# Eight gate tiles of a hybrid decoder layer computed in earlier stages and kept in DRAM instead of in the last stage

## The chip, the cores and the metric

The kernel runs on one core of a Trainium2 chip. The metric is the device time of one execution in microseconds (us), lower is better. One execution in each set is taken with the hardware profiler; its rows are what the argument below rests on.

## What is computed

One inference step of one layer for 520 tokens (a prompt of 512 and 8 samples), model width 1024, everything in float32. The reference, cut to what matters:

```python
x = layer_norm(x_in, ln_in_g, ln_in_b)
xm, ig, fg, og, zm, rcols, zr, u, zs, gm = split_cols(x @ w_in)
y_A = mlstm(xm, ig, fg, og) * silu(zm) @ w_bm     # chunkwise, 4 heads of 256
y_B = rwkv7(rcols) * silu(zr) @ w_br              # 16 heads of 64, state by token
y_C = glu(gelu(s5(u))) * silu(zs) @ w_bs          # 64 groups of 64 complex states
g0, g1, g2 = split(sigmoid(gm), 3)
x = layer_norm(ALPHA * x + (g0 * y_A + g1 * y_B + g2 * y_C) @ w_out, ln_g, ln_b)
```

The change is about `g0`, the merge gate of the mLSTM branch: 1024 of the columns of `x @ w_in`, in eight tiles of 128 columns.

## The kernel before, in words

**Products.** A float32 product is made of three matmuls on split operands: `x` is kept as `xh` + `xl` and a weight tile as `whi` + `wlo`, and the terms hi x hi, lo x hi and hi x lo are added in PSUM. A tile of 128 output columns by 520 tokens is 8 slices of the inner dimension x 3 terms x 2 token halves (256 and 264) = 48 matmuls. `inproj(c0, evac)` makes one tile of `x @ w_in` so. `load_w` fetches the tile in two halves (`wraw`, three buffers); ACT rounds each half to `whi` (L130), DVE takes the rest as `wlo` (L131). `whi` and `wlo` have two buffers.

**Stages.** The program runs RWKV (to about 727 us), S5 with the RWKV output branch beside it (to about 940 us), mLSTM with the S5 output branch beside it (to about 1203 us), then the last stage: gating of the mLSTM output, the product with `w_bm`, and `final()` with the product by `w_out` and the closing layer norm (L1652 ff.). A generator of one stage is interleaved with that of another by `interleave`; within this, a scheduler that works on its own model of time sets the order of the instructions on each engine, and each engine then runs its list in that order. All loads and stores are issued by one queue, SP (SyncE), also in a fixed order: a transfer that waits for its buffer or its data holds up all that are behind it.

**Kept products ("fills").** RWKV's chain over chunks of the prompt leaves PE waiting, so tiles of `x @ w_in` that later stages need are computed there ahead of time: 44 of them stand in the list `fills`. `fill_z` runs `inproj`, copies the tile from PSUM to `zf` (DVE, one copy for each token half) and stores it in DRAM (`zsave`, 260 KB a tile). 25 are made between other products of RWKV; the other 19 are issued at the end of `rwkv()` by `e.fill(len(e.fills))` (L796) and the scheduler spreads them from there.

**The users.** `Merge.gate` (L1551) has two ways: if its columns stand in `zsave` it loads the tile by DMA and applies Tanh, otherwise it calls `inproj`. In the last stage `Merge.other(0, ahead=True)` calls it for the eight tiles of `g0`, which are not among the 44, so they are computed there, on PE, each tile between two columns of the gating: `zz` (kept `zm`) is loaded, `th` = Tanh, `yb` (the mLSTM output, `hmsave`) is loaded, multiplied and split into `w_bmh` and `w_bml`, the operands of the product with `w_bm`. That product needs all eight columns. Its result is scaled by the gate (`gt`, L1587, DVE) and added to `mg` (L1588, POOL).

**xh and xl.** These hold the normalised input for as long as a tile of `x @ w_in` is still to be made. After that the last stage loads the raw normalised rows into the same memory (`xr`, `xg`, from `xsave`, 2 MB) and scales them on POOL for the residual (L1682, ten instructions of 1024 columns).

**Names on the path of RWKV's end.** `cr`, `cy`: matmuls of the chain over the eight chunks; `hm`, `hv`: means and variances of the head norm behind it; `bv`: its result, stored as `ybsave`. S5 then loads `pk`, `uu`, `br`, `cc`, and its first DVE instruction is `bb<-br,pk` (L1000). At S5's end `ss` (DVE) is the last state, `ys` (PE) the last output product, `yssave<-yo` its store, and the S5 branch loads it again as `yb` and splits it into `ysh` and `ysl`.

Of the kernel before, what the change touches and what calls it, by code (L numbers as in the profile page):

```python
# [8 lines left out]
F32 = mybir.dt.float32  # L9
# [6 lines left out]
P = 128  # L16
# [3 lines left out]
N = T + NB  # L20
# [12 lines left out]
EH = math.exp(-0.5)  # L33

C_XM, C_IG, C_FG, C_OG, C_ZM = 0, 1024, 1028, 1032, 2056
C_RC, C_ZR, C_U, C_ZS, C_GM = 3080, 6280, 7304, 8328, 9352


@with_exitstack
def hybrid_step(ctx: ExitStack, tc: tile.TileContext, I, O):  # L40
# [225 lines left out]
    hmsave = dr.tile([KT, P, N], F32, name="hmsave")  # L266
    ud = dr.tile([KT, P, SL, 80], F32, name="ud")
    flc = ExitStack()
    fl = flc.enter_context(tc.tile_pool(name="fl", bufs=1))
    zsave, fills = {}, []  # L270

    def fill_u(ct):
        us = fl.tile([P, SL, 80], F32, tag="fl", bufs=2, name="us")
# [41 lines left out]
    for ct in range(2):  # L315
        fills.append((fill_z, (C_GM + D + ct * P, zd[ct])))

    def fill(k=1):
        for _ in range(k):
            if fills:  # L320
                f, c = fills.pop(0)
                f(c)
# [36 lines left out]

    env = dict(locals())  # L360
    rwkv(tc, I, O, env)
    flc.close()
    mrg = Merge(tc, I, O, env)
    weng[:] = [V, V]
    mrg.open("mr", 1, 4)
    interleave(s5(tc, I, O, env), mrg.other(1), 1.5)
    mrg.pctx.close()
    weng[:] = [V, V]
    mrg.open("ms", 1, 4)
    interleave(mlstm(tc, I, O, env), mrg.s5(), 0.42)  # L370
    mrg.pctx.close()
    mrg.open("mf", 3, 5)
    for _ in mrg.other(0, ahead=True):
        pass
# [6 lines left out]
def interleave(a, b, n):  # L381

    due = 0.0
    for _ in a:
        due += n
        while due >= 1:
            next(b, None)
            due -= 1
    for _ in b:
        pass  # L390


def rwkv(tc, I, O, env):
# [239 lines left out]
    def chain(cts, st):  # L633
        yr = rq.tile([P, 2, T], F32, tag="yr", bufs=1, name="yr")
        st_fin = rq.tile([P, 2, RD], F32, tag="stf", bufs=1, name="stf")
        yv, t1, lr, pcs = st["yv"], st["t1"], st["lr"], st["pc"]
        xv = rq.tile([P, 2, 2, RD], F32, tag="xv", bufs=2, name="xv")
        for pi in range(2):
            G.memset(xv[hs(pi), pi], 0.0)
        for n in range(NCH):  # L640
            b1, b2 = pc("cr"), pc("cy")
            q3 = lambda b, j: b[:, 128 * j:128 * j + 128].rearrange("p (c t) -> p c t", c=2)
            pr_, psa_, py, psn = q3(b1, 0), q3(b1, 1), q3(b2, 0), q3(b2, 1)
            if n < NCH - 1:
                nxv = rq.tile([P, 2, 2, RD], F32, tag="xv", bufs=2, name="xv")
            for pi in range(2):
                G.tensor_copy(xv[hs(1 - pi), pi], yv[hs(1 - pi), pi, :, n, :])  # L647
            for ci, pi in heads:
                mm(pr_[hs(pi), ci, :], st["ar"][ci][:, pi, n, 0:CH], xv[:, pi, ci, :])
            rs = rss[n % 2]  # L650
            A.activation(rs[hs(0), 0], pr_[hs(0)], AF.Copy)
            V.tensor_copy(rs[hs(1), 1], pr_[hs(1)])
            for ci, pi in heads:
                mm(psa_[hs(pi), ci, :], t1[:, :, ci * NCH + n], rs[:, pi, ci, :])
            V.tensor_copy(yv[hs(0), 0, :, n, :], psa_[hs(0)])
            A.copy(yv[hs(1), 1, :, n, :], psa_[hs(1)])
            for ci, pi in heads:
                mm(psn[hs(pi), ci, :], st["bkt"][ci][:, pi, n, :], yv[:, pi, ci, n, :])
            for ci, pi in heads:
                dst = nxv[hs(pi), pi, ci, :] if n < NCH - 1 else st_fin[hs(pi), ci, :]  # L660
                V.scalar_tensor_tensor(dst, xv[hs(pi), pi, ci, :], pcs[ci][hs(pi), n:n + 1], psn[hs(pi), ci, :],  # L661
                                       op0=ALU.mult, op1=ALU.add)
            for ci in range(2):
                for pi in range(2):
                    mm(py[hs(pi), ci, :], xv[:, pi, ci, :], st["ar"][ci][:, pi, n, CH:2 * CH], stop=False)
                for pi in range(2):
                    mm(py[hs(pi), ci, :], yv[:, pi, ci, n, :], lr[:, pi, ci * NCH + n, :], start=False)
            A.activation(yr[:, :, n * CH:(n + 1) * CH], py, AF.Copy)
            if n < NCH - 1:
                xv = nxv  # L670
        for ci in range(2):
            p = pc("wf")
            tr(p[0:64, 0:P], st_fin[:, ci, :])
            wo = rq.tile([64, P], F32, tag="wo", bufs=1, name="wo")
            V.tensor_copy(wo, p[0:64, 0:P])
            for pi in range(2):
                dma(O[10][0, 0, 2 * cts[ci] + pi], wo[:, 64 * pi:64 * pi + 64])
        return yr
# [114 lines left out]
    V.tensor_tensor(yst, yst, lng, op=ALU.mult)  # L793
    V.tensor_tensor(bf, bf, yf, op=ALU.add)
    dma(e.ybsave[:, :, T:N].rearrange("c p b -> p c b"), bvs)
    e.fill(len(e.fills))  # L796
    ctx2.close()
    ctx.close()
    e.weng[:] = [V, V]
# [145 lines left out]
def s5(tc, I, O, env):  # L945
# [20 lines left out]
    for pi in range(KT // 2):  # L966
# [48 lines left out]
        for j in range(2):  # L1015
            c0 = g0 + 8 * j
            eb = sp.tile([P, 8, SL, SC], F32, tag="eb", bufs=2, name="eb")
            et = sp.tile([P, 8, SL, SC], F32, tag="et", bufs=2, name="et")
            pw = lambda t, q, lo_: t[:, q, lo_:lo_ + SL, c0:c0 + 8].rearrange("p s g -> p g s").unsqueeze(3).to_broadcast(sh)
            bx = lambda q: bb[:, q, 8 * j:8 * j + 8].unsqueeze(2).to_broadcast(sh)  # L1020
            V.tensor_tensor(eb, pw(pf, 0, 0), bx(0), op=ALU.mult)
            V.tensor_tensor(et, pw(pf, 1, 0), bx(1), op=ALU.mult)
            V.tensor_tensor(eb, eb, et, op=ALU.add)
            gm = sp.tile([P, 8, SL, SC], F32, tag="gm", bufs=2, name="gm")
            cx = lambda q: ca[:, j, q].unsqueeze(2).to_broadcast(sh)
            V.tensor_tensor(gm, pw(pf, 0, 1), cx(0), op=ALU.mult)
            gt = sp.tile([P, 8, SL, SC], F32, tag="et", bufs=2, name="gt")
            V.tensor_tensor(gt, pw(pf, 1, 1), cx(1), op=ALU.mult)
            V.tensor_tensor(gm, gm, gt, op=ALU.add)


            p = pa("ko")
            for m in range(4):
                mm(p[32 * m:32 * m + 32, 0:2 * P], ca[:, j, 0, 2 * m:2 * m + 2, :].rearrange("p g c -> p (g c)"),
                   eb[:, 2 * m:2 * m + 2].rearrange("p g s c -> p (g s c)"))
            kt = sp.tile([P, 2, P], F32, tag="w4", bufs=6, name="kt")
            A.activation(kt.rearrange("p h c -> p (h c)"), p[:, 0:2 * P], AF.Copy)
            p = pa("kt")
            for h in range(2):
                tr(p[:, h * P:(h + 1) * P], kt[:, h])  # L1040
            for h in range(2):
                A.activation(ko[:, j].rearrange("p (m h c) -> p m h c", h=2, c=SC)[:, :, h],
                             p[:, h * P:(h + 1) * P].rearrange("p (m h c) -> p m h c", h=2, c=SC)[:, :, h], AF.Copy)
            gms.append(gm)
            ebs.append(eb)
        kf = ko.rearrange("p j c -> p (j c)")
        V.tensor_tensor(kf[0:SC], kf[0:SC], dm.rearrange("p g c -> p (g c)"), op=ALU.add)
        for t in range(SL):
# [695 lines left out]
```

## Time and profile before

| | |
|---|---|
| median of 3 runs | 1374.99 us |
| lowest, highest | 1374.82, 2058.82 us |
| profiled execution | 1377.44 us |
| span of its trace | 1375.5 us |
| matmul engine (PE) busy | 1248.1 us, 91% of the span, 10509 instructions |
| VectorE (DVE) busy | 990.8 us, 72% |
| ScalarE (ACT) busy | 643.8 us, 47% |
| GpSimd (POOL) busy | 241.5 us, 18% |
| mean granted clock of PE | 0.953 of full speed |

The highest of the three runs stands far off from the other two, which differ by 0.17 us; the median is beside the lower ones. The profiled execution is 2.45 us above the median. Busy shares are means over stages that have different limits, so the stages are read apart: by windows of the trace, by the chain of waits that ends last, and by the timeline of a single engine.

### The profile page before, as it was taken

How to read it: one execution, taken by the hardware profiler on the slowest of the kernel's cores; microseconds unless marked ns; L12 is line 12 of the kernel's file. 1: busy time of each engine (PE TensorE's matmuls, PEld its weight loads, DVE VectorE, ACT ScalarE, POOL GpSimd, SP SyncE). 2: the span in 40 equal slices, each digit the busy share in tenths (PEclk: the TensorE clock that was granted, in tenths of full speed). 3: DMA queues.
4: the chain of work that ended last, by engine and by line, in shares of the span. 5: the costliest groups of instructions: out<-in, count | busy, mean ns of one | idle time of the engine just before them, and what ended most of it. 6: DMA issues, size and time to landing. Idle time of an engine off the chain costs nothing.

```text
span 1375.5 us, 27646 instructions
## 1 busy us (share of the span) xinstructions
PE 1248.1 (91%) x10509; PEld 1141.7 (83%) x10509; DVE 990.8 (72%) x2245; ACT 643.8 (47%) x1404; POOL 241.5 (18%) x396
## 2 busy tenths in 40 slices
PE   4979989998999999999985999996999999999897
PEld 4979988888888888998965889985889888899855
DVE  6795695558567945688936999994776775665857
ACT  4447647364846573342222433333665774453230
POOL 1412211122112221105100002200000012104600
PEclk9989999999998999999977999996999999999999
DMA  6333232222221312354417554464676866475331
GB/s 185 95 109 101 81 97 67 56 63 61 80 77 40 95 55 71 88 170 131 153 44 141 136 104 111 100 160 134 196 230 206 264 201 209 134 218 172 90 110 63
DMA packets 246707, 168.49 MB, mean 122 GB/s; under 512 B 54808, under 2 KB 222106, under 8 KB 246302
## 3 DMA queue, kind: packets, MB, share of 16 engines
q1 hardware_dynamic: 246574, 166.72, 42.9%
q8 instruction: 83, 1.36, 0.4%
q14 instruction: 50, 0.41, 0.1%
HBM read 125.18 MB, written 39.20 MB: 120 GB/s over the span
## 4 chain that ended last, share of the span: by engine, by line
PE 60%; DVE 15%; ACT 8%; DMA 8%; issue 5%; SPq 3%; POOL 0%; DVEq 0%; ACTq 0%
PE g L62 40%; SPq L53 3%; DVE wlo L131 3%; PE ys L62 2%; PE cy L62 2%; PE cr L62 2%; PE qk L62 2%; PE gg L62 1%; PE nd L62 1%; PE s L62 1%; DMA wraw<-in_w_bm_dram 1%; ACT whi L130 1%; PE pn L62 1%; DMA uu<-ud 1%; ACT bk L573 1%
## 5 line engine op out<-in xcount | busy, mean ns | idle before, releaser
L62 PE MATMUL g<-xh,whi 128*128 128x264 f32 (+1 forms) x1552 | 458.5, 296 | 35.8 <-DVE th L1541 14.4
L62 PE MATMUL g<-xl,whi 128*128 128x264 f32 (+1 forms) x1552 | 455.3, 293 | 1.9 <-DVE xl L217 1.9
L62 PE MATMUL g<-xh,wlo 128*128 128x264 f32 (+1 forms) x1552 | 455.0, 293 | 0.6 <-DVE wlo L131 0.4
L62 PEld LDWEIGHTS g<-xh,whi 128*128 128x128 f32 x1552 | 303.1, 195 | 44.5 <-DVE th L1541 15.5
L62 PEld LDWEIGHTS g<-xl,whi 128*128 128x128 f32 x1552 | 303.0, 195 | 4.7 <-DVE xl L217 2.2
L62 PEld LDWEIGHTS g<-xh,wlo 128*128 128x128 f32 x1552 | 302.6, 195 | 4.4 <-DVE wlo L131 1.1
L130 ACT ACTIVATE whi<-wraw 128x512 fp32r<-128x512 f32 x258 | 150.8, 624 | 235.7 <-PE g L62 168.7
L131 DVE TENSOR_TENSOR wlo<-wraw,whi 128x512 fp32r<-128x512 f32 x258 | 201.6, 809 | 56.5 <-ACT whi L130 55.5
L661 DVE SCALAR_TENSOR_TENSOR xv<-xv,pc,cy 64x64 f32<-64x64 f32 x112 | 31.3, 280 | 31.0 <-PE cy L62 28.1
L62 PE MATMUL g<-ysh,whi 128*128 128x256 f32 (+1 forms) x128 | 39.0, 314 | 13.1 <-ACT ysh L258 10.7
L62 PE MATMUL g<-w_bmh,wlo 128*128 128x264 f32 (+1 forms) x128 | 37.3, 293 | 8.2 <-DVE wlo L131 8.1
L599 DVE TENSOR_TENSOR itmp<-lu,xi 128x31 f32<-128x31 f32 (+15 forms) x124 | 42.2, 340 | 2.9
L601 DVE TENSOR_TENSOR xi<-xi,itmp 128x31 f32<-128x31 f32 (+15 forms) x124 | 42.2, 341 | 2.7
L564 DVE TENSOR_TENSOR lr<-gg,maskg 64x256 f32<-64x256 f32 x32 | 13.5, 422 | 42.6 <-ACT la L563 37.3
L647 POOL COPY xv<-yv 64x128 f32<-64x128 f32 x64 | 25.9, 406 | 103.8 <-PE cy L62 56.6
L62 PE MATMUL g<-ysl,whi 128*128 128x256 f32 (+1 forms) x128 | 39.8, 312 | 0.0
L62 PE MATMUL g<-ysh,wlo 128*128 128x256 f32 (+1 forms) x128 | 38.9, 305 | 0.0
L62 PEld LDWEIGHTS g<-ysh,whi 128*128 128x128 f32 x128 | 26.0, 209 | 14.6 <-ACT ysh L258 10.9
L62 PE MATMUL g<-bsh,whi 128*128 128x264 f32 (+1 forms) x128 | 37.8, 301 | 0.0
L62 PE MATMUL g<-bsl,whi 128*128 128x264 f32 (+1 forms) x128 | 37.3, 293 | 0.0
L62 PE MATMUL g<-bsh,wlo 128*128 128x264 f32 (+1 forms) x128 | 37.0, 291 | 0.0
L62 PE MATMUL g<-w_bmh,whi 128*128 128x264 f32 (+1 forms) x128 | 36.9, 289 | 0.0
(583 smaller groups left out, 2948.4 us busy)
## 6 DMA issues: line engine op xcount, KB each, us to landing
wraw<-in_w_in_dram SPq DMA_DIRECT2D x194, 256.0 KB
zsave<-zf SPq DMA_DIRECT2D x36, 260.0 KB
cn<-in_state_mlstm_c_dram SPq DMA_DIRECT2D x32, 256.0 KB
out_dram<-cn SPq DMA_DIRECT2D x32, 256.0 KB
yb<-yssave SPq DMA_DIRECT2D x16, 260.0 KB
zz<-zsave SPq DMA_DIRECT2D x16, 260.0 KB
wraw<-in_w_br_dram SPq DMA_DIRECT2D x16, 256.0 KB
wraw<-in_s_glu_w_dram SPq DMA_DIRECT2D x16, 256.0 KB
```

Source lines behind the costliest of these rows:

```text
L53: nc.sync.dma_start(out, in_)
L62: TE.matmul(out, lhsT, rhs, start=start, stop=stop)
L130: A.activation(hi[:, k, 0:m], raw[:, :, 0:m], AF.Copy)
L131: eng.tensor_tensor(lo[:, k, 0:m], raw[:, :, 0:m], hi[:, k, 0:m].bitcast(F32), op=ALU.subtract)
L564: V.tensor_tensor(lr[hs(pi), pi, u, :], pv[hs(pi), :, 64:128], maskg[hs(pi)].unsqueeze(1).to_broadcast([64, 4, 64]), op=ALU.mult)
L573: A.activation(bk[:, n], bk[:, n], AF.Copy, scale=st["pc"][ci][:, n:n + 1])
L599: V.tensor_tensor(tv, lu[:, s + 1:32, s:s + 1].to_broadcast([P, r, w]), xi[:, s:s + 1, 0:w].to_broadcast([P, r, w]), op=ALU.mult)
L601: V.tensor_tensor(xi[:, s + 1:32, 0:w], xi[:, s + 1:32, 0:w], tv, op=ALU.add)
L647: G.tensor_copy(xv[hs(1 - pi), pi], yv[hs(1 - pi), pi, :, n, :])
L661: V.scalar_tensor_tensor(dst, xv[hs(pi), pi, ci, :], pcs[ci][hs(pi), n:n + 1], psn[hs(pi), ci, :], op0=ALU.mult, op1=ALU.add)
```

## The change

Eight more entries are appended to `fills`, the tiles `C_GM + ct*128` of `g0` with a DRAM buffer `zsave6`. Of the list's last part, all but five tiles are issued at the end of `rwkv()` as before; two more are issued there too, but tied by `tc.issue_after` behind the last matmul of RWKV's chain (`st["last"]`, a `cy<-yv,bkt`); the last three (`LATE`) are issued in S5's companion generator `beside()` after the RWKV branch, tied behind the last transpose of S5's last group (`marks[-1]`). The pool of `zf` stays open until after mLSTM and moves to the right side of the memory. `Merge.gate` is unchanged: its first way is now taken in the last stage.

```diff
+LATE = 3
-    fl = flc.enter_context(tc.tile_pool(name="fl", bufs=1))
-    zsave, fills = {}, []
+    fl = flc.enter_context(tc.tile_pool(name="fl", bufs=1, side="right"))
+    zsave, fills, marks = {}, [], []
+    zd = dr.tile([KT, P, N], F32, name="zsave6")
+    for ct in range(KT):
+        fills.append((fill_z, (C_GM + ct * P, zd[ct])))
     rwkv(tc, I, O, env)
-    flc.close()
-    interleave(s5(tc, I, O, env), mrg.other(1), 1.5)
+    def beside():
+        yield from mrg.other(1)
+        with tc.issue_after(marks[-1]):
+            fill(len(fills))
+        yield
+    interleave(s5(tc, I, O, env), beside(), 1.5)
     interleave(mlstm(tc, I, O, env), mrg.s5(), 0.42)
     mrg.pctx.close()
+    flc.close()
     mrg.open("mf", 3, 5)
@@ rwkv, the chain's step
-                mm(psn[hs(pi), ci, :], st["bkt"][ci][:, pi, n, :], yv[:, pi, ci, n, :])
+                st["last"] = TE.matmul(psn[hs(pi), ci, :], st["bkt"][ci][:, pi, n, :], yv[:, pi, ci, n, :],
+                                       start=True, stop=True)
@@ rwkv, its end
-    e.fill(len(e.fills))
+    e.fill(len(e.fills) - LATE - 2)
+    with tc.issue_after(st["last"].ins):
+        e.fill(2)
@@ s5, for each group
-                tr(p[:, h * P:(h + 1) * P], kt[:, h])
+                last = TE.transpose(p[:, h * P:(h + 1) * P], kt[:, h], e.ident)
+            e.marks.append(last.ins)
```

The number of matmuls stays the same; 384 of them change their place. How the order of instructions moves is shown at three places.

**SP at the end of RWKV.** Before, the queue runs from the last weight loads of RWKV to S5's first loads:

```order
L53 DMA ysb<-ys_d 8x1024
L53 DMA wraw<-in_w_in_dram 128x4x128 x2
L53 DMA ybsave<-bvs 128x8x8
L53 DMA out_dram<-wo 64x64 x4
L53 DMA ybsave<-bv 128x512 x2
L53 DMA pk<-pksave 128x2080
L53 DMA uu<-ud 16x16x80 x8
```

After the change, from the same place on (the stores `zsave_340` are those of the new buffer):

```order
L54 DMA wraw<-in_w_in_dram 128x4x128 x2
L54 DMA out_dram<-wo 64x64 x4
L54 DMA zsave_340<-zf 128x520
L54 DMA wraw<-in_w_in_dram 128x4x128 x2
L54 DMA ybsave<-bv 128x512
L54 DMA zsave_340<-zf 128x520
L54 DMA wraw<-in_w_in_dram 128x4x128 x2
L54 DMA ybsave<-bv 128x512
L54 DMA wraw<-in_w_in_dram 128x4x128 x2
L54 DMA pk<-pksave 128x2080
L54 DMA uu<-ud 16x16x80 x8
```

The load of `pk`, which S5 begins with, now stands behind the stores of kept tiles and behind further pairs of weight loads. On PE the moved matmuls (240 for five tiles) lie as follows: 72 in the sixth of the chain's eight steps (before, these three places held none of them), 128 among the `wf`, `hm` and `hv` matmuls between the chain's last `cy` and the last `hv`, and 40 behind the last `hv`.

**PE at the end of S5.** Before, near the last group's last output products, PE has tiles of the S5 branch (`g<-ysh`) between them:

```order
L62 MATMUL ys<-uu,tm 128x72 x2
L62 MATMUL g<-ysh,whi 128x256
L62 MATMUL g<-ysl,whi 128x256
L62 MATMUL g<-ysh,wlo 128x256
L62 MATMUL g<-ysh,whi 128x256
```

After, in the same place:

```order
L63 MATMUL ys<-uu,tm 128x72 x2
L63 MATMUL g<-xh,wlo 128x264
L63 MATMUL g<-xh,whi 128x264
L63 MATMUL g<-xl,whi 128x264
L63 MATMUL g<-xh,wlo 128x264
```

All 144 matmuls of the three late tiles stand ahead of the last `ys<-ss`, and 38 matmuls of the S5 branch have gone from before it to behind it (52 stood there, now 14). The DVE list has four `wlo` and four `zf` copies more ahead of the last `ss`.

**POOL, the residual's scaling.** Before, its ten instructions stand among the additions `mg<-mg,gt` of the last stage:

```order
L1588 TENSOR_TENSOR mg<-mg,gt 128x256
L1682 TENSOR_TENSOR xr<-xr,xg 128x1024
L1682 TENSOR_TENSOR xg<-xg 8x1024
L1682 TENSOR_TENSOR xr<-xr,xg 128x1024 x3
L1588 TENSOR_TENSOR mg<-mg,gt 128x264
L1682 TENSOR_TENSOR xr<-xr,xg 128x1024
```

After, they stand among the additions `mg<-mg,gth` of the S5 branch, that is, in the mLSTM stage, near the second of its eight tiles:

```order
L1604 TENSOR_TENSOR mg<-mg,gth 128x64x4
L1698 TENSOR_TENSOR xr<-xr,xg 128x1024
L1698 TENSOR_TENSOR xg<-xg 8x1024
L1698 TENSOR_TENSOR xr<-xr,xg 128x1024 x3
L1604 TENSOR_TENSOR mg<-mg,gth 128x64x4
L1604 TENSOR_TENSOR mg<-mg,gth 128x8
L1698 TENSOR_TENSOR xr<-xr,xg 128x1024
L1350 COPY xcs<-xc 128x8
```

Their loads move with them on SP, because `xh` and `xl` are read for the last time at the end of S5's companion work and the last `x @ w_in` tiles of mLSTM and no longer in the last stage. In the last stage PE's list goes from the S5 branch straight to the 384 matmuls with `w_bm` (before: 384 of `x @ w_in`, then these), the first 72 of them ordered by column over three tiles; SP's has the loads `zz`, four `gt`, `yb`, `zz`, four `gt`, `yb` and then `zz` and `yb` in turn, without weight loads of `w_in` between them.

## Rows read from the trace of the kernel before

**Rows 1.** Page, part 1: busy time, share of the span, instructions

```profile
PE 1248.1 (91%) x10509; PEld 1141.7 (83%) x10509; DVE 990.8 (72%) x2245; ACT 643.8 (47%) x1404; POOL 241.5 (18%) x396
```

**Rows 2.** Chain that ended last, its long pieces: start, length (us), what

```profile
1202.75 46.91 PE g L62 x391
...
1310.82 54.77 PE g L62 x254
```

**Rows 3.** Windows by stage: window, length; busy PE, PEld, DVE, ACT, POOL; PEclk, DMA, GB/s

```profile
697.00:740.00 43.00, 26.98 (x210) 20.96 (x208) 12.07 (x35) 12.51 (x34) 4.12 (x9) 0.73 0.41 66
740.00:934.00 194.00, 180.74 (x1613) 172.04 (x1614) 189.91 (x371) 68.42 (x143) 23.36 (x23) 0.94 0.53 120
905.00:940.00 35.00, 32.09 (x272) 30.42 (x270) 29.16 (x72) 11.45 (x23) 0.92 (x4) 0.85 0.43 116
940.00:951.00 11.00, 0.48 (x4) 0.20 (x2) 2.33 (x13) 0.52 (x1) 0.92 (x3) 0.60 0.60 132
1110.00:1130.00 20.00, 20.00 (x137) 17.50 (x139) 18.85 (x60) 13.04 (x29) 3.48 (x6) 1.00 0.65 199
1130.00:1203.00 73.00, 73.00 (x526) 60.76 (x515) 41.29 (x126) 35.42 (x70) 12.50 (x18) 1.00 0.55 173
1250.00:1311.00 61.00, 49.66 (x385) 47.99 (x384) 46.26 (x43) 16.47 (x29) 39.19 (x25) 0.94 0.45 136
```

**Rows 4.** DVE's wlo in 1110 to 1203 us: count, ns min/median/max

```profile
L131 DVE TENSOR_TENSOR wlo<-wraw,whi x14: 684/690/1248, 1115.7 to 1201.6; 128x512 fp32r<-128x512 f32 x14
```

**Rows 5.** DVE's wlo in 1250 to 1311 us: count, ns min/median/max

```profile
L131 DVE TENSOR_TENSOR wlo<-wraw,whi x14: 684/1243/8168, 1250.2 to 1299.7; 128x512 fp32r<-128x512 f32 x14
```

**Rows 6.** Timeline of DVE in the last stage: start, length, instruction, count

```profile
1241.65 0.69 DVE L262 SCALAR_TENSOR_TENSOR w_bml<-yb,w_bmh 128x520 fp32r<-128x520 f32 x1
...
1271.44 0.75 DVE L1587 SCALAR_TENSOR_TENSOR gt<-gt,g 128x256 f32<-128x256 f32 x2
1272.11 11.02 DVE L131 TENSOR_TENSOR wlo<-wraw,whi 128x512 fp32r<-128x512 f32 x2
```

**Rows 7.** Windows of 10 us at the end of RWKV's chain, columns of rows 3

```profile
700.00:710.00 10.00, 6.35 (x76) 5.07 (x74) 3.63 (x14) 1.43 (x6) 0.58 (x2) 0.67 0.06 6
710.00:720.00 10.00, 8.29 (x44) 5.31 (x44) 1.97 (x7) 2.57 (x8) 1.86 (x2) 0.50 0.04 7
```

**Rows 8.** Timeline of PE, end of RWKV: start, length, instruction [idle before]

```profile
722.76 1.13 PE L62 MATMUL hv<-yq,bones 128*128 128x256 f32 x4 [1.72 <-ACT yq L688]
```

**Rows 9.** Timeline of SP's queue, RWKV to S5

```profile
723.05 3.90 SPq L53 DMA_DIRECT2D ybsave<-bv  x2
727.04 0.38 SPq L53 DMA_DIRECT2D pk<-pksave  x1
727.47 5.99 SPq L53 DMA_DIRECT2D uu<-ud  x8
...
735.16 2.83 SPq L53 DMA_DIRECT2D br<-in_s_b_im_dram  x2
```

**Rows 10.** Timeline of DVE, start of S5

```profile
740.23 0.42 DVE L1000 TENSOR_TENSOR bb<-br,pk 128x256 f32<-128x256 f32 x1 [6.38 <-DMA br<-in_s_b_im_dram]
```

**Rows 11.** Timeline of PE, first matmul behind the end of S5

```profile
951.17 0.58 PE L62 MATMUL g<-ysh,whi 128*128 128x256 f32 x1 [10.69 <-ACT ysh L258]
```

**Rows 12.** POOL by line and shape: count, busy us, mean ns, idle before

```profile
L1682 POOL TENSOR_TENSOR xr<-xr,xg 128x1024 f32<-128x1024 f32 x8 | 20.8, 2607 | 0.7 <-DMA xg<-in_ln_in_g_dram 0.7
...
L1682 POOL TENSOR_TENSOR xg<-xg 8x1024 f32<-8x1024 f32 x2 | 4.7, 2356 | 0.0
```

**Rows 13.** Timeline of POOL in the mLSTM stage

```profile
1119.32 1.24 POOL L1588 TENSOR_TENSOR mg<-mg,gth 128x256 f32<-128x256 f32 x1 [2.31 <-DVE r L1282]
```

**Rows 14.** Timeline of SP's queue, start of the last stage

```profile
1204.64 3.96 SPq L53 DMA_DIRECT2D out_dram<-so  x10
...
1209.74 0.45 SPq L53 DMA_DIRECT2D zz<-zsave  x1
```

## The prediction, made from the rows above

> **What bounds the kernel now.** PE is busy for 91% of the span [rows 1], and the change neither adds nor removes a matmul. It moves 384 of them, so the question is what limits each of the stages that give or take them. I read the windows by stage first, then the chain that ended last at the two ends of the change, then the timelines of single engines there.
>
> The last stage gives. Its eight gate tiles are one piece of 46.91 us and 391 matmuls of the chain, 0.120 us each, and nothing but PE is waited for [rows 2]. The product with w_bm follows, and at 1310.82 the product with w_out. That middle window, 1250 to 1311, has 385 matmuls, 46.2 us of work at that rate, but takes 61 [rows 3]; what it loses is seen on DVE: two wlo take 11.02 us, where the same instruction has a median of 0.69 in mLSTM [rows 4 to 6].
>
> Three stages take. At RWKV's end the chain over chunks waits and PE's clock is low: between 700 and 720 PE is busy for 14.64 us of 20 at a granted clock of 0.67 and then 0.50 [rows 7]. S5 from 740 to 934 has DVE busy for 189.91 of 194 us: DVE is its bound [rows 3]. mLSTM has PE busy throughout and, from 1110 to 1130, DVE for 18.85 of 20 [rows 3].
>
> **The change part by part.** All against the profiled execution of 1377.44 us (span 1375.5), which lies 2.45 above the median.
>
> *RWKV's end, five tiles, 240 matmuls, 28.8 us at 0.120.* 200 of them (24.0 us) stand ahead of the last hv, which before ends at 722.76 + 1.13 = 723.9 [rows 8]. What can hide them: PE's idle time of 3.65 + 1.71 us in 700 to 720, the 1.72 us that hv waits [rows 7, 8], and the clock, which steady work would raise: 6.35 x 0.33 + 8.29 x 0.50 = 6.2 us. Together 13.3; so hv ends 10.7 us later. Behind it stands the store of bv, and behind that on SP, now, two more pairs of weight loads and a store ahead of pk; before, pk came 3.99 us after the issue of the bv stores began, with nothing between [rows 9]. A weight load waits for its buffer, which the fifth tile's 40 matmuls behind hv free only as they run, 4.8 us at most; I take 4. Everything that S5 begins with is queued there: pk, eight uu, four br. These take 13.2 us from pk at 727.04 to bb at 740.23, and bb waits for the last of them [rows 9, 10]; they are needed as before, only later. bb then starts near 755. S5 can't catch up, since DVE has 4 us of idle time in 194 [rows 3]: **+15**. Bounds: +8 if the buffers are free and idle time before 700 and after 720 hides a little more; 28.8 if nothing hides. I choose near the low clock's rows, because they lie exactly where the matmuls go.
>
> *S5's end, three tiles, 144 matmuls.* All come before the last ys, 38 of the S5 branch go behind it: 106 x 0.120 = 12.7 us more ahead of it. In 905 to 940 PE has 2.91 us of idle time and loses 32.09 x 0.15 = 4.8 by the clock [rows 3]; 5.0 remain. By DVE it is alike: four wlo at 0.69 [rows 4] and four zf copies, taken like wlo as an upper bound, are 5.5 us ahead of the last ss. The two run beside each other, so I take **+5** (bounds 2 and 12.7). What follows is not shortened: after the last ys the result goes to DRAM and back, and PE's first matmul waits 10.69 us for it [rows 11]. The 38 matmuls that went behind fall into that gap, where PE is busy for 0.48 of 11 us [rows 3], and cost nothing; without the gap they would be 4.6 us. Three zsave stores stand on SP ahead of yssave; a single store's issue takes under 0.5 us, as pk's does [rows 9], and they are in the 5.
>
> *mLSTM, POOL's ten instructions.* They take 20.8 + 4.7 = 25.5 us [rows 12]. Since xh and xl are free earlier, they now follow POOL's mg addition of 1119.32 [rows 13], in the stage where DVE is 94% busy until 1130 and 57% (41.29 of 73) after it, and where PE never waits [rows 3]. In the last stage wlo beside them went from 0.69 up to 8.17 us, and two in a row took 11.02, while two gt, which read PSUM, stayed at 0.75 [rows 4 to 6]. That stage lost 61 - 46.2 = 14.8 us. In mLSTM only the first third falls into the crowded part, and PE's list holds three streams of work to draw on; I take half, **+7**. Bounds: 0, if every stalled DVE result was early enough, and 23.5, if POOL's 25.5 us are lost to DVE less the 1.15 + about 1 us free in the crowded part.
>
> The Trainium skill's page "SBUF — State Buffer", section "SBUF: two separate sides", says that DVE and GpSimd share a port pair, held as an exclusive lock for a whole instruction, and that a DVE operation with two SBUF inputs against a GpSimd operation that reads SBUF blocks fully. The trace agrees: wlo, with two SBUF inputs, has 8.17 us, and gt, with one operand in PSUM, has not [rows 5, 6]. By that rule the move would cost close to the upper bound wherever DVE is the bound, and it speaks against this change: by it the sum would be that of rival B, 1384, by the half that I take 1370.
>
> *Last stage, 46.9 us of matmuls gone.* The time doesn't fall by that, because the product with w_bm needs the gating, which ran beside them: zz is loaded from 1209.74 and the eighth w_bml ends at 1241.65 + 0.69 = 1242.3 [rows 6, 14], eight columns in 32.6 us, each a chain of DMA, ACT and DVE. The weight loads of w_in between the columns go, 1 MB of gate loads for each four columns come; SP's stores end at 1204.64 + 3.96 = 1208.6 as before [rows 14]. I take the chain to end at about 1238. PE meanwhile does only what columns are ready: the first 72 matmuls are ordered by column, so 63 of them can be done. Then 321 remain, 38.5 us at 0.120 [rows 2], since POOL's instructions no longer hold wlo up, and about 2.5 for the clock after idle time (5 us at half the clock; the stretch of 0.50 in [rows 7] shows the level). The end is 1238 + 38.5 + 2.5 = 1279 instead of 1310.8: **-32**. Bounds: -38 with the columns 6 us earlier, -25 with them 7 us later (the gate loads ahead of yb). Gate loads and Tanh, eight of each, lie beside this.
>
> Sum: 15 + 5 + 7 - 32 = -5. 1377.44 - 5 = 1372.4, and on the median's basis (2.45 lower) **1370 us**.
>
> **The rivals.**
>
> *A, the tiles hide.* The windows with low clock and idle time speak for it [rows 7]; the queue order on SP and DVE's 189.91 of 194 in S5 speak against. RWKV +8, S5 +2, mLSTM 0, last stage -35: -25, 1352 on the profile's basis, 1350 on the median's.
>
> *B, POOL's instructions block DVE in mLSTM at nearly full price.* DVE's 94% there speaks for it [rows 3], as do the stretched wlo [rows 5, 6]; that only 14 wlo lie in those 93 us [rows 4], and that DVE has 43% free after 1130, speak against. With 21 us in place of 7 the sum is +9: 1386, or 1384. The result is slower than before as soon as the block costs more than 12 us, the others as taken.
>
> *C, RWKV's end hides nothing*, since the 72 matmuls stand inside the chain's sixth step and 128 in the norm, where every step waits for DVE results that PE makes possible. RWKV 28.8, S5 12.7, mLSTM 7, last stage -25: +23.5, 1401, or 1398. Against it: the clock of 0.50 [rows 7].
>
> That the gates are still computed in the last stage is excluded by the order of instructions.
>
> **How the numbers follow.** My own case has 0.5 (1362 to 1378 for it alone), A 0.2, B 0.2, C 0.1. The range goes from A's 1350, a little lower for its spread, to above B's 1384, leaving out C: 1349 to 1388. A difference of 2% is about what a measurement of this kernel can tell from no change, 27.5 us: below 1347.5 only the better part of A, 0.08; above 1402.5 the worse part of C, 0.04; within, 0.88.
>
> **What would show it.** In the changed kernel's profile: hv's end near 735 and the first bb near 755 (A: under 749, C: near 768); DVE still over 95% busy through S5; the last ys and yssave about 20 us later than before; PE's 10.7 us wait behind it unchanged. In mLSTM, wlo or other DVE instructions with two SBUF operands of several us beside POOL's ten, and PE waits that add up to about 7 (B: 20). In the last stage, a PE that is mostly idle for about 30 us while zz, th, yb and w_bml run, then 384 matmuls ending some 41 us after the last w_bml, with wlo at 0.69. The prediction is wrong if S5 recovers the delay of its start, which would need DVE work of its first chain to have been waiting for something other than DVE, or if the gating finishes early, near 1225, which would give 13 us more.

## The result and the profile after

The changed kernel takes 1390.92 us (median of 4 runs, 1390.24 to 1394.38), 1.0094 times the kernel before, with a 95% interval of 1.0077 to 1.0111. The ratio is taken over fast executions of both kernels alone and is not the quotient of the two medians printed here (1390.92 / 1374.99 = 1.0116). The changed kernel is slower by 0.9%, and its time lies above the predicted range, 1349 to 1388. The profiled execution took 1390.24 us with a span of 1388.5, 12.8 and 13.0 us above those of the kernel before.

The reading goes by five marks: the first bb (S5 starts), the beginning of the last stores of yssave (S5 ends), the first zz (the last stage starts), the start of the product with w_out, and the end. For the product with w_out the mark is the start of the chain's long last piece, 254 matmuls; two more w_out matmuls begin 1.2 us before it in both kernels. From the changed kernel, SP's queue (start, length, instruction), DVE and the long pieces of the chain that ended last:

```profile
742.92 0.50 SPq L54 DMA_DIRECT2D pk<-pksave  x1
961.05 5.37 SPq L54 DMA_DIRECT2D yssave<-yo  x9
1253.71 0.45 SPq L54 DMA_DIRECT2D zz<-zsave  x1
```

```profile
757.04 0.42 DVE L1015 TENSOR_TENSOR bb<-br,pk 128x256 f32<-128x256 f32 x1 [7.87 <-DMA br<-in_s_b_im_dram]
1283.67 0.70 DVE L263 SCALAR_TENSOR_TENSOR w_bml<-yb,w_bmh 128x520 fp32r<-128x520 f32 x1 [0.70 <-ACT w_bmh L259]
```

```profile
1325.43 53.21 PE g L63 x254
```

| from one mark to the next | before | after | difference | predicted |
|---|---|---|---|---|
| start to first bb | 740.23 | 757.04 | +16.8 | +15 |
| to yssave | 199.8 | 204.0 | +4.2 | +5 |
| to first zz (mLSTM) | 269.7 | 292.7 | +22.9 | +7 |
| to the product with w_out | 101.1 | 71.7 | -29.4 | -32 |
| to the end | 64.7 | 63.1 | -1.6 | 0 |
| sum | | | +13.0 | -5 |

The marks before are from [rows 2, 10, 14] and, for yssave, this row of SP's queue in the kernel before:

```profile
940.02 4.33 SPq L53 DMA_DIRECT2D yssave<-yo  x9
```

Four of five terms lie within 3 us of what the sum had for them. The mLSTM stage does not. Windows of the changed kernel there (window, length; busy PE, PEld, DVE, ACT, POOL; PEclk, DMA, GB/s):

```profile
1132.00:1152.00 20.00, 20.00 (x141) 17.18 (x140) 19.02 (x56) 10.76 (x23) 6.17 (x5) 1.00 0.92 316
1152.00:1175.00 23.00, 9.72 (x43) 6.86 (x42) 20.42 (x16) 8.00 (x15) 21.05 (x14) 0.71 0.24 75
1175.00:1225.00 50.00, 50.00 (x340) 39.91 (x339) 27.02 (x71) 21.14 (x44) 9.48 (x13) 0.96 0.66 209
```

PE, which had no idle time from 1110 to 1203 in the kernel before [rows 3], works for 9.72 of 23 us, at a granted clock of 0.71, while POOL is busy for 21.05. The timeline shows POOL first, then DVE:

```profile
1148.03 2.37 POOL L1698 TENSOR_TENSOR xr<-xr,xg 128x1024 f32<-128x1024 f32 x1 [4.98 <-DMA xg<-in_ln_in_g_dram]
1150.35 2.40 POOL L1698 TENSOR_TENSOR xg<-xg 8x1024 f32<-8x1024 f32 x1
1152.73 7.54 POOL L1698 TENSOR_TENSOR xr<-xr,xg 128x1024 f32<-128x1024 f32 x3
...
1165.92 4.76 POOL L1698 TENSOR_TENSOR xr<-xr,xg 128x1024 f32<-128x1024 f32 x2
```

```profile
1150.67 2.12 DVE L1313 TENSOR_TENSOR sc<-mv,r 128x4 f32<-128x4 f32 x1
1153.36 2.27 DVE L132 TENSOR_TENSOR wlo<-wraw,whi 128x512 fp32r<-128x512 f32 x1 [0.57 <-ACT whi L131]
1155.55 2.32 DVE L1314 TENSOR_TENSOR sc<-sc,r 128x4 f32<-128x4 f32 x1
...
1161.17 9.66 DVE L1426 TENSOR_SCALAR hT<-hT,mv,sc 128x256 f32<-128x256 f32 x4
```

The instructions `sc` and `hT` are the head norm of mLSTM. `sc`, 128x4 elements, takes 2.12 and 2.32 us, nearly as long as one POOL instruction, and four `hT` take 9.66. In the kernel before the same stretch begins and ends with:

```profile
1129.04 0.16 DVE L1297 TENSOR_TENSOR sc<-mv,r 128x4 f32<-128x4 f32 x1
...
1133.64 1.38 DVE L1410 TENSOR_SCALAR hT<-hT,mv,sc 128x256 f32<-128x256 f32 x4
```

The durations of hT over the whole trace, before and then after (line, count, ns min/median/max):

```profile
L1410 DVE TENSOR_SCALAR hT<-hT,mv,sc x16: 402/407/414, 1019.6 to 1195.3; 128x256 f32<-128x256 f32 x16
```

```profile
L1426 DVE TENSOR_SCALAR hT<-hT,mv,sc x16: 407/409/2586, 1041.5 to 1238.7; 128x256 f32<-128x256 f32 x16
```

What waits for them is PE, for the transposes `ht` (what waits, for what in 1132 to 1180: us in total, times, longest):

```profile
PE ht L82 <- DVE hT L1426: 12.6, 4, 7.2
```

These 12.6 us are nearly all of the 13.28 us that PE idles in the window of 23 us. The rest of the 22.9 is not split up here; a part of it is the granted clock, which is 0.71 in this window and 0.96 in the 50 us behind it, against 1.00 in the kernel before [rows 3].

### The profile page after: what moved, and what is told of

It is laid out like the page before. It is cut to its first block, busy times and chain, and to the rows that moved or that the text cites. A ratio compares the mean times of both kernels' runs of the same rounds, so it can differ in the third digit from the quotient of the medians.

```text
span 1388.5 us, 27681 instructions
## 1 busy us (share of the span) xinstructions
PE 1249.1 (90%) x10509; PEld 1140.9 (82%) x10509; DVE 995.2 (72%) x2261; ACT 644.7 (46%) x1396; POOL 234.9 (17%) x396
## 4 chain that ended last, share of the span: by engine, by line
PE 56%; DVE 17%; DMA 11%; ACT 9%; issue 4%; SPq 2%; POOL 0%; DVEq 0%; ACTq 0%; POOLq 0%
PE g L63 39%; DVE wlo L132 3%; SPq L54 2%; PE cr L63 2%; PE ys L63 2%; PE gg L63 1%; ACT whi L131 1%; PE cy L669 1%; DMA zz<-zsave 1%; DMA wraw<-in_w_in_dram 1%; PE pn L63 1%; DMA wraw<-in_w_bs_dram 1%; ACT bk L584 1%; PE s L63 1%; PE qk L63 1%
## 5 line engine op out<-in xcount | busy, mean ns | idle before, releaser
L132 DVE TENSOR_TENSOR wlo<-wraw,whi 128x512 fp32r<-128x512 f32 x258 | 181.8, 732 | 42.3 <-ACT whi L131 41.0
L63 PE MATMUL g<-w_bmh,whi 128*128 128x256 f32 (+1 forms) x128 | 36.8, 312 | 19.1 <-ACT w_bmh L259 19.1
L299 DVE COPY zf<-g 128x256 f32<-128x256 f32 x72 | 30.4, 424 | 19.5 <-PE g L63 18.7
L63 PEld LDWEIGHTS g<-w_bmh,whi 128*128 128x128 f32 x128 | 24.8, 207 | 21.6 <-ACT w_bmh L259 21.3
L63 PE MATMUL g<-w_bml,whi 128*128 128x256 f32 (+1 forms) x128 | 39.6, 311 | 0.3 <-DVE w_bml L263 0.2
L63 PE MATMUL g<-w_bmh,wlo 128*128 128x256 f32 (+1 forms) x128 | 38.3, 302 | 0.0
```

The source lines that it names most:

```text
L63: TE.matmul(out, lhsT, rhs, start=start, stop=stop)
L132: eng.tensor_tensor(lo[:, k, 0:m], raw[:, :, 0:m], hi[:, k, 0:m].bitcast(F32), op=ALU.subtract)
L299: V.tensor_copy(z[:, s:s + n], p)
```

## The experiments

Theory L: POOL's ten scaling instructions lock DVE out in the mLSTM stage, and the whole of the loss there is this. Theory D: the residual's loads, 3 MB that now stand ahead of weight loads on SP, make it; for this speaks a piece of 12.82 us in the chain, `DMA wraw<-in_w_bs_dram` from 1139.85, a few us before the stretch above. The runs went to several chips. The kernel before ran beside each group (1381.31 us beside e1, e2, e4 and e7, medians of 1378.27 beside e5, e6, e8 and e9 and of 1377.83 beside e7b, e10, e11 and e12); the changed kernel did not. e1, e2, e4, e5, e7 and e10 are single executions, the others 4 to 10. Inside a trace the stretches between the marks say more than totals. All of them, in us:

| kernel | first bb | yssave | yssave to zz | zz to w_out | span |
|---|---|---|---|---|---|
| before | 740.23 | 940.02 | 269.7 | 101.1 | 1375.5 |
| changed | 757.04 | 961.05 | 292.7 | 71.7 | 1388.5 |
| e1, loads and POOL late | 757.68 | 962.55 | 270.4 | 82.4 | 1378.7 |
| e2, POOL late | 760.67 | 965.07 | 270.6 | 84.7 | 1385.9 |
| e4, scaling on DVE behind the gating | 759.63 | 964.45 | 273.8 | 85.6 | 1388.7 |
| e9, scaling on DVE in mLSTM | 759.60 | 965.29 | 282.8 | 71.5 | 1382.8 |
| e10, no scaling | 760.47 | 964.53 | 274.0 | 72.8 | 1374.5 |
| e11, scaling on DVE late in w_bm | 758.38 | 963.33 | 272.1 | 79.1 | 1380.6 |
| e5, only RWKV's five | 762.18 | 962.84 | 268.2 | 97.5 | 1391.6 |
| e6, only S5's three | 740.30 | 942.50 | 277.4 | 96.2 | 1379.2 |
| e8, S5's three, scaling on DVE | 737.19 | 939.88 | 278.7 | 95.3 | 1377.0 |
| e7, before, scaling on DVE behind the gating | 737.62 | 937.62 | 269.7 | 95.1 | 1365.5 |
| e7b, the same, six executions | 740.34 | 940.06 | 271.2 | 94.8 | 1369.1 |
| e12, before, scaling on DVE late in w_bm | 737.61 | 937.10 | 270.7 | 95.0 | 1368.8 |

Kernels that are alike up to the first bb differ there by up to 3.1 us without RWKV's five and by up to 5.1 with them, so single totals are read no finer than that. In e11 and e12 the long last piece has 256 matmuls and so begins with the first of w_out: their 79.1 and 95.0 are about 1 us too low beside the other rows.

### Loads and POOL back in the last stage

```diff
+        with self.tc.issue_after(self.ld.ins):        # last yb<-hmsave, on SP
             dma(xr, e.xsave[0:T]...); dma(xg[0:NB, 2], ...); dma(xg[:, j], ...)
+                        with self.tc.issue_after(self.adds[-14].ins):   # third mg<-mg,gt, on POOL
                             G.tensor_tensor(x[:n], x[:n], xg[:n, j], op=op)
```

> The changed kernel, but the residual's loads (xr, xg, 3 MB) are tied behind the last hmsave load of the gating, and POOL's ten scaling instructions behind the third addition mg<-mg,gt, so both stand in the last stage again as in the kernel before. From the first store of yssave to the first load of zz takes 269.7 us in the kernel before (940.02 to 1209.74) and 292.7 in the changed one (961.05 to 1253.71). Theory L (POOL's ten instructions lock DVE out in the mLSTM stage) and theory D (the 3 MB of loads delay the weight loads that stand behind them on SP): both expect 270 to 272 here, and stretched wlo in the product with w_bm once more, some 10 us of it; total about 1380 us. A third theory R, that neither matters and the mLSTM stage is longer because it started from another state of the queues: 290 or more, total over 1395.

Measured: 1380.47 us beside 1381.31; yssave to zz 270.4, zz to w_out 82.4. Both as L and D expect; the mLSTM stage has its old length, and R is out. The last stage shows the lock again: of the 29.4 us that it gained in the changed kernel, 10.7 (82.4 less 71.7) came from POOL's work and the residual's loads having left it.

### Only POOL back, the loads early

The second half of the diff above alone.

> The changed kernel with POOL's ten scaling instructions tied behind the third addition mg<-mg,gt of the last stage; the 3 MB of loads stay where the change put them, in the mLSTM stage. Theory L: from the first yssave to the first zz about 273 us (292.7 in the changed kernel), total about 1380. Theory D: about 285 or more, since the weight loads of w_bs still wait behind the 3 MB (the piece of 12.82 us in the chain), total about 1395. If both share, in between, and the two stretches say how much each has.

Measured: 1387.59 us; yssave to zz 270.6, as with both moved. The 3 MB still stand ahead of the w_bs loads here and cost nothing that this mark shows. The hT rows are back to their old size:

```profile
L1426 DVE TENSOR_SCALAR hT<-hT,mv,sc x16: 405/409/415, 1044.8 to 1221.6; 128x256 f32<-128x256 f32 x16
```

The total is over L's 1380 because of other stretches: the first bb is 3.6 us later than in the changed kernel, and zz to w_out has 84.7, with a wlo of up to 6.67 us there. With POOL's work alone back, the last stage loses 13.0 of its 29.4 us (84.7 less 71.7).

### No scaling at all

```diff
-                    for j, op in enumerate((ALU.mult, ALU.add)):
-                        G.tensor_tensor(x[:n], x[:n], xg[:n, j], op=op)
```

> The changed kernel without POOL's ten scaling instructions: the residual is then added unscaled, and this work is left out. Loads and all else stay as in the change. Theory L (the lock is the whole of the mLSTM stage's loss): from yssave to zz 269 to 271 us (292.7 in the changed kernel), zz to the first w_out matmul 71 to 73 as in the changed kernel, total 1366 to 1370. Theory D (loads): yssave to zz 275 or more, since the 3 MB still stand ahead of the w_bs loads.

Measured: 1376.43 us; yssave to zz 274.0, zz to w_out 72.8. The stage loses its hole:

```profile
1150.00:1175.00 25.00, 24.12 (x168) 18.54 (x167) 14.45 (x44) 16.61 (x34) 3.85 (x8) 1.00 0.83 276
```

PE 24.12 of 25 us and DVE 14.45. By e10 the lock costs 292.7 - 274.0 = 18.7 us, by e2 22.1. Up to 4.3 us, in e10, may belong to the loads (theory D asked for 275 or more), but e2 has them too and shows 0.9. So L has at least four fifths of the 22.9, and D the rest at most. The long wait for a w_bs load, which spoke for D, stands in e10's chain too:

```profile
1143.79 12.54 DMA wraw<-in_w_bs_dram
```

It is as long as the 12.82 us of the changed kernel, and the stage is 18.7 us shorter all the same. The total is 6 to 10 us over what was expected: 3.5 of them stand ahead of yssave, which came later than in the changed kernel by that much, and 3 to 5 in the mLSTM stage, where 269 to 271 were expected.

### The scaling on DVE

```diff
-                        G.tensor_tensor(x[:n], x[:n], xg[:n, j], op=op)
+                        with self.tc.issue_after(self.gd.ins):     # eighth yb<-yb,th of the gating
+                            V.tensor_tensor(x[:n], x[:n], xg[:n, j], op=op)
```

In the changed kernel (e4), and, with the tie behind the third S5 tile of the mLSTM stage (e9) or behind the eleventh gate multiplication (e11):

> The changed kernel with the ten scaling instructions of the residual on DVE in place of POOL, tied behind the eighth gating product (yb<-yb,th), loads early as in the change. On DVE a 128x1024 product of two SBUF operands takes 1.22 us by S5's rows (eb<-pk,bb), so ten take 12 us, beside the product with w_bm where DVE is idle a third of the time. Theory L: mLSTM as in the kernel before (from yssave to zz 270 to 274 us), no stretched wlo, total 1370 to 1374. Theory D: from yssave to zz 285 or more, total 1385 or more.

> The changed kernel (all eight tiles kept, loads early) with the ten scaling instructions on DVE, tied behind the third tile of the S5 branch in the mLSTM stage, where POOL did them near there in the changed kernel. Theory L: on DVE they cost at most their own 12 us there, not 22, and less where DVE is idle: yssave to zz 272 to 282 (292.7 with POOL), zz to the first w_out matmul 71 to 74, as in the changed kernel; total 1371 to 1381 against 1390. Theory D or a plain overload of DVE in that stage: yssave to zz 288 or more, total 1386 or more.

> The changed kernel with the ten scaling instructions on DVE, tied behind the eleventh of the sixteen gate multiplications of the last stage, so that they stand at the end of the product with w_bm, where all weight splits for it are done. Theory L: no lock anywhere and little DVE work in the way: yssave to zz 270, zz to the first w_out matmul 72 to 76, total 1368 to 1375, that is 0 to 0.7% under the kernel before: what the change is worth once the lock is out of it. If DVE's 12 us there hold up PE as in the version tied behind the gating (85.6 us from zz): 1380 or more.

Measured: e4 1390.56 us in a single execution; e9 1.0026 (1.0008 to 1.0043) and e11 1.0054 (1.0037 to 1.0071) of the kernel before. In e4 the mLSTM stage is mended (273.8), but what was won goes in the last stage, 85.6: five of the ten stand ahead of the last w_bml, which every further matmul with w_bm waits for, and five ahead of the next wlo.

```profile
1266.56 0.70 DVE L263 SCALAR_TENSOR_TENSOR w_bml<-yb,w_bmh 128x520 fp32r<-128x520 f32 x1
1268.60 1.22 DVE L1699 TENSOR_TENSOR xr<-xr,xg 128x1024 f32<-128x1024 f32 x1
1269.73 1.21 DVE L1699 TENSOR_TENSOR xg<-xg 8x1024 f32<-8x1024 f32 x1
1270.87 3.48 DVE L1699 TENSOR_TENSOR xr<-xr,xg 128x1024 f32<-128x1024 f32 x3
1274.27 0.68 DVE L263 SCALAR_TENSOR_TENSOR w_bml<-yb,w_bmh 128x520 fp32r<-128x520 f32 x1
1274.88 1.21 DVE L1699 TENSOR_TENSOR xr<-xr,xg 128x1024 f32<-128x1024 f32 x1
...
1277.15 3.48 DVE L1699 TENSOR_TENSOR xr<-xr,xg 128x1024 f32<-128x1024 f32 x3
1281.56 2.00 DVE L132 TENSOR_TENSOR wlo<-wraw,whi 128x512 fp32r<-128x512 f32 x2
```

The expectation of 1370 to 1374 was wrong: DVE's own 12 us count where they stand in the way. In e9 the ten take about 1.2 us each and yssave to zz has 282.8, just over the upper end of what was expected, and about half of POOL's price. e11 is a miss too (79.1 where 72 to 76 was expected): PE works for 17.27 us of the 24 in which DVE does the scaling:

```profile
1290.00:1314.00 24.00, 17.27 (x128) 16.68 (x126) 23.15 (x30) 7.00 (x13) 12.33 (x6) 0.91 0.32 91
```

In the changed kernel none of the three places on DVE makes the scaling free.

### The same edit in the kernel before

> The kernel before with the ten scaling instructions on DVE, tied behind the eighth gating product. Measures what POOL's instructions cost in the last stage of the kernel before by themselves. Theory L: the window of the product with w_bm (61 us for 46.2 us of matmuls) shrinks to about 50, total 1366 to 1368 against 1377.4 of the profiled execution. If the 14.8 us lost there are from something else (late weight loads of w_bm, 10.98 us in the chain), it stays within 3 us of the kernel before.

> The kernel before with the scaling on DVE behind the eighth gating product, timed now (one look gave 1367.4 beside 1381.3). Theory L: 0.5 to 1.0% under the kernel before, zz to the first w_out matmul about 95 us.

> The kernel before with the same edit, scaling on DVE at the end of the product with w_bm. Theory L: zz to the first w_out matmul 101.1 us before, 88 to 92 here (the 14.8 us lost there go, less some DVE work), total 1363 to 1368, 0.7 to 1.1% under the kernel before. If the stretch was lost to late weight loads of w_bm: 98 to 101, no difference.

Measured: e7 1367.42 us beside 1381.31, a single execution of each; over six executions (e7b) 0.9940 of the kernel before (0.9921 to 0.9958), and behind the eleventh gate multiplication (e12) 0.9949 (0.9931 to 0.9968). Both beat both kernels. zz to w_out is 94.8 and 95.1 instead of 101.1 in e7b and e7, and about 96 in e12: exchanging the lock for DVE's own 12 us is worth 5 to 6 us there. That e7's total fell into the 1366 to 1368 that were expected is luck: the stretch gave 6 us of the 11 that were to go, and the first bb came 2.6 us earlier than in the kernel before, where nothing was changed. e12 was expected at 88 to 92, as if DVE's work were nearly free; how much of the remaining stretch is DVE's and how much the weight loads' was not separated.

### One place at a time

Only RWKV's five (`LATE = 0`, three entries fewer in the list), and only S5's three (no tied pair at RWKV's end; e6, and e8 with the scaling on DVE behind the gating):

```diff
-    for ct in range(KT):
+    for ct in range(KT - 3):       # e5; in e6 range(3), and no e.fill(2) behind st["last"]
         fills.append((fill_z, (C_GM + ct * P, zd[ct])))
```

> Only the five tiles at RWKV's end are kept; the other three are made in the last stage as before (so xh and xl stay in use and POOL's scaling stays in the last stage). Gives the price of RWKV's end by itself. If the price is that of the changed kernel: first bb near 757 (before 740.2), yssave near 957, 270 us from there to zz, and the last stage (zz to the first matmul with w_out, 101.1 us before, 82.4 with all eight kept and POOL's scaling late) at 83 to 88, since three tiles, 17.5 us of PE, fit beside the 31 us of gating: total 1376 to 1381. If S5's end is where the delay comes from and RWKV's end hides its tiles: bb under 748, total under 1370.

> Only the three tiles at S5's end are kept, none more in RWKV; five are made in the last stage as before. Price of S5's end by itself: first bb near 740, yssave near 944 to 945 (before 940.0), 270 us to zz. The last stage is to show how much of the eight tiles the gating hides anyway: five tiles are 29 us of PE beside about 31 us of gating. If they hide: zz to the first w_out matmul 84 to 90, total 1366 to 1371, about 0.6% under the kernel before. If every tile made there costs its 5.8 us: 101.1 - 17.5 = 84 without the gating as a limit, or about 96 where the gating and the tiles don't overlap, total 1375 to 1378.

> As the kernel with three tiles at S5's end, and the ten scaling instructions of the residual on DVE, tied behind the eighth gating product. The same edit took 14 us from the kernel before in one look (1367.4 beside 1381.3) and nothing from the changed kernel where it stands ahead of weight splits that PE waits for. Theory L: no stretched wlo; 6 to 12 us less than the kernel with POOL's scaling: total 1356 to 1364, 1.0 to 1.6% under the kernel before. If DVE's own 12 us in the product with w_bm are as bad as the lock: 1366 to 1371.

Measured: e5 1393.7 us; first bb 762.18, and from bb to yssave 200.7 (before 199.8): the price of RWKV's end is the five tiles' and S5 doesn't recover it. e6 1.0013 (0.9992 to 1.0035); bb at 740.30, and bb to yssave 202.2, so S5's three tiles cost 2.4 us. The other half of the expectations failed: with three or five tiles left in the last stage, zz to w_out is 95 to 97. e5 was expected at 83 to 88; e6, at 84 to 90 if its tiles hide, lies at its other alternative, 96. From yssave to zz, e6 and e8 take 277.4 and 278.7, with some 46 matmuls more between these marks than the kernel before has (1885 and 1839), so the two stretches are better read as one: from yssave to w_out e6 takes 373.6 us, the kernel before 370.8. The order puts all remaining tiles of w_in ahead of the product with w_bm, and the residual's loads, which wait for the last of them, now stand ahead of the last loads of the gating. From e6, SP and DVE:

```profile
1244.06 0.37 SPq L54 DMA_DIRECT2D xr<-xsave  x1
1246.10 0.33 SPq L54 DMA_DIRECT2D yb<-hmsave  x1
...
1248.95 3.83 SPq L54 DMA_DIRECT2D xg<-in_ln_in_g_dram  x1
...
1253.35 0.38 SPq L54 DMA_DIRECT2D yb<-hmsave  x1
```

```profile
1255.64 0.70 DVE L1651 TENSOR_TENSOR yb<-yb,th 128x520 f32<-128x520 f32 x1 [6.17 <-DMA yb<-hmsave]
...
1262.87 2.06 DVE L263 SCALAR_TENSOR_TENSOR w_bml<-yb,w_bmh 128x520 fp32r<-128x520 f32 x1 [0.70 <-ACT w_bmh L259]
...
1271.04 14.11 DVE L132 TENSOR_TENSOR wlo<-wraw,whi 128x512 fp32r<-128x512 f32 x2
```

The seventh yb is issued behind the 2 MB of xr, and the issue of another of the residual's loads takes 3.83 us with the last yb behind it. DVE waits 6.17 us for the seventh yb and 2.87 more for the eighth, the gating ends 45 us after zz (1262.87 + 2.06, less 1219.89; 30.7 in the changed kernel), and then two wlo take 14.11 us beside POOL's scaling. So keeping three tiles instead of eight saves nothing. In e5 the loads come earlier still, DVE waits 8.90 us for the third yb, and POOL's scaling falls on the gating itself. Instructions of the gating, before POOL begins and beside it:

```profile
1240.76 0.70 DVE L1562 SCALAR_TENSOR_TENSOR th<-th,zz 128x520 f32<-128x520 f32 x1 [0.60 <-ACT th L1561]
1241.38 0.70 DVE L263 SCALAR_TENSOR_TENSOR w_bml<-yb,w_bmh 128x520 fp32r<-128x520 f32 x1
...
1257.72 2.84 DVE L1562 SCALAR_TENSOR_TENSOR th<-th,zz 128x520 f32<-128x520 f32 x1
1260.48 2.83 DVE L263 SCALAR_TENSOR_TENSOR w_bml<-yb,w_bmh 128x520 fp32r<-128x520 f32 x1
```

In e8 the lock is gone, but the late gating stays, and five of the ten scaling instructions stand on DVE ahead of its last w_bml, which ends 46.7 us after zz: 1.0045 (1.0028 to 1.0062) where 1356 to 1371 us were expected.

## Why the prediction was wrong, by its steps

**What bounds each stage** held. The last stage behaved as described: the gating took 1284.37 - 1253.71 = 30.7 us (28 were foreseen, 1238 - 1209.74), PE was busy for 16.83 of them, and w_out began 41.1 us after the last w_bml (41 foreseen).

**RWKV's end**, +15, came out at +16.8, with its parts shifted. The last hv ended at 738.6 instead of 734.6:

```profile
720.00:730.00 10.00, 10.00 (x85) 9.55 (x85) 3.01 (x7) 3.11 (x8) 1.87 (x2) 0.94 0.26 73
730.00:740.00 10.00, 10.00 (x78) 9.73 (x77) 3.43 (x7) 5.16 (x11) 0.00 (x0) 1.00 0.39 119
```

```profile
737.98 0.59 PE L63 MATMUL hv<-yq,bones 128*128 128x256 f32 x2
```

Less was hidden (PE is busy for all 20 us from 720 to 740), the queue behind hv cost 1.2 us and not 4, and from pk to bb it took 0.9 us more than before. That the term came out near is in part luck: errors of 4.0 and 2.8 us had opposite signs. bb was foreseen near 755 and came at 757.04. In the runs on other chips it came between 757.7 and 762.2 with RWKV's five, and between 737.2 and 740.3 without them.

**S5's end**, +5, was +4.2, and 2.4 and 2.9 without RWKV's five (e6, e8).

**The last stage**, -32, was -29.4. It is made of two parts: 18.7 us from the tiles and 10.7 from the scaling that left by e1 (101.1 to 82.4, and 82.4 to 71.7), 16.4 and 13.0 by e2 (84.7 in between).

**mLSTM** is the step that failed: "That stage lost 61 - 46.2 = 14.8 us. In mLSTM only the first third falls into the crowded part, and PE's list holds three streams of work to draw on; I take half, +7." The mechanism was named, and rival B had the direction in which the result went; the size was 18.7 to 22.1 for the lock (e10, e2), three times the value taken and close to the upper bound of 23.5. The argument went by DVE's busy share and by wlo, which is made ahead of its use: PE waited for no wlo in this stage. It did not ask which other DVE instructions stand in the stretch and who waits for them. They were the head norm's sc and hT, a chain of short instructions between PE's products and PE's transposes: the two sc shown and each of the four hT were held until a POOL instruction had ended, so the stretch from the first sc to the last hT, 6.0 us before (1129.04 to 1135.02), became 20.2 (1150.67 to 1170.83). The three streams did not help either: PE runs its list in order, and the list had ht next.

With the measured 22.9 in place of 7 the sum is +11, 1388 us of a profiled execution, or rival B's neighbourhood; the remaining 2 us are the small errors of the other terms. Rival B's point of decision, 12 us, was nearly right: with the other terms as measured it is 10. B, given 0.2, is what came; the half taken in its place was a choice, not worked out from a row.

The Trainium skill's page "SBUF — State Buffer", section "SBUF: two separate sides", counts among what competes for the shared port also DVE operations in its two-port modes, beside those with two SBUF inputs. hT has one tensor input in SBUF and two scalars for each partition, and was held (2.59 us for 0.41); the prediction looked only for instructions with two tensors. The views don't name an instruction's mode, but durations in the kernel before speak for a two-port one: such a TENSOR_SCALAR takes 0.41 us with 256 columns (hT) and 0.80 with 1024 (xin, L195), 0.51 ns for each further column, while instructions with two inputs take 0.69 with 512 (wlo) and 1.22 with 1024 (eb, L1021), 1.04 ns. That it is the mode for which hT was held is not shown.

**Theory D fell** as a main cause: with the loads early and POOL late (e2), the stage had its old length to 0.9 us. A share of up to 4.3 us remains possible by e10.

**What the change is worth without the lock** is little or nothing. No version of it that does all the work is faster than the kernel before by more than single executions differ: e1 has 1380.47 us beside 1381.31, and e9 is 1.0026 of the kernel before. On one chip, the kernel with kept tiles and without scaling (e10) has 72.8 from zz to w_out, and the kernel before with the scaling on DVE (e7b) 94.8: 22 us won, with the scaling left out of e10 altogether; but its yssave stands 24.5 us later (964.53 against 940.06). The gain of the last stage is paid at RWKV's and S5's end, before the lock is counted.

## What to carry to other kernels

When work that is moved frees a buffer earlier, list everything that waits for the buffer: here ten instructions and 3 MB of loads moved by a whole stage without a line of theirs in the diff, and the ten instructions made the difference. Price such a neighbour by the short instructions on a chain that another engine waits for, not by the busy share of the engine it disturbs. And where a wide elementwise job sits on POOL beside a busy DVE, try it on DVE before moving other work: in the kernel before that alone gave 0.5 to 0.6%. In the changed kernel none of the places tried brought it under the kernel before.

## What the runs showed of the hardware that was not expected

In these traces a DVE instruction with two SBUF operands that begins beside a POOL instruction on SBUF operands ends only behind it, however small it is: `sc` of 128x4 elements, 0.16 us in the kernel before, ran from 1150.67 to 1152.79 beside POOL's `xg`, which ended at 1152.75. Where POOL's instructions follow close upon each other, one DVE instruction can be held by several: in the kernel before the wlo of 8.17 us [rows 5], from 1274.96, lies beside four:

```profile
1274.45 2.84 POOL L1682 TENSOR_TENSOR xr<-xr,xg 128x1024 f32<-128x1024 f32 x1
1277.26 2.34 POOL L1682 TENSOR_TENSOR xg<-xg 8x1024 f32<-8x1024 f32 x1
1279.57 0.71 POOL L1588 TENSOR_TENSOR mg<-mg,gt 128x256 f32<-128x256 f32 x1
1280.24 2.33 POOL L1682 TENSOR_TENSOR xr<-xr,xg 128x1024 f32<-128x1024 f32 x1
```

DVE instructions that read PSUM (`hT<-gt,nd`, 0.41 us at 1148.37 in the changed kernel, POOL busy from 1148.03) and the norm's statistics (`bs<-hT`, 0.43 at 1148.82) were not held. `xg`, of 8 partitions, took POOL as long as 128 (2.40 and 2.37 us), and DVE did the same 128x1024 product in 1.2 us.
